# Second layer of a two-layer trunk: output projection by token halves, first products of the MLP and the input projection after it, operands ahead, stores on other queues

## The chip, the cores and the metric

The kernel runs on one core of a Trainium2 chip. The metric is the device time of one execution, in microseconds, as the median of three runs. The core has five engines that run their own instruction streams: TensorE (PE), VectorE (DVE), ScalarE (ACT), GpSimd (POOL) and SyncE (SP), which issues DMAs; ACT and POOL can issue DMAs too. They meet through semaphores, and each runs its instructions in the order of its stream.

## The reference

One sequence of 1024 tokens, model width 1024, float32. Layer 0 has attention, layer 1 a recurrent and convolution mixer; both end in an output projection. What matters here is the tail of each layer:

```
h = h + y @ w_out[i]                                   # output projection
hn = rms_norm(h, norm_mlp[i])
h = h + square(relu(hn @ w_mlp_in[i])) @ w_mlp_out[i]  # hidden width 4096
hn = rms_norm(h, norm_ple[i])
h = h + (p[i] @ w_ple_proj[i]) * sigmoid(hn @ w_ple_gate[i])   # p: 1024 x 256
...
return rms_norm(h, norm_final)
```

## The kernel before

Activations are held transposed: features on 128 partitions (8 blocks, `h[0]` to `h[7]`), 1024 tokens along the free axis, which splits into a left half (`lt`, tokens 0 to 511) and a right half (`rt`). `P` is 128, `H` 512, `T` 1024, `KB` 8.

Every float32 product is made of three matmuls of reduced operands (`mm3`, lines L95 to L97): an operand is split into a high part `xh` by ACT (`hi`, L76) and a low part `xl` by DVE (`lo`, L79 or L89 for weights, L155 with a gain), and PE adds high x high, high x low and low x high in one bank of its accumulator memory. Each matmul is 128 x 128 weights against 512 columns. Weights (`wr`, `raw`) come in blocks of 512 KB through two buffers, and their split parts (`wh`, `wl`) go through three.

The stages of layer 1, in order: the recurrent mixer; the output projection (`out_proj`, which calls `blocks`): 8 tiles of output features, two halves each; the norm (`rstd_full`) and `up_operands`; `mlp_up`; `mlp_down`; `ple_last`. Both parts of the MLP use seven products in place of eight (the Winograd form of Strassen's scheme, P1 to P7): `mlp_up` works on pairs of hidden tiles (16 pairs, index `mp`), and X1 to X7, sums and differences of quarters of the normed h, are its operands, `x10h` being the high part of block 0 of X1. A pair takes 84 matmuls, 12 for each product. Of its weights the sums `s12` and `s34` are split into `sh` and `sl`, and the last quarter into `ah`, `al`. A pair's results `z1` and `z2` (after relu and square) and the differences `tt` are stored to memory (`oa`, `ob`, `ot`), and `mlp_down` loads them again (`zr`), splits them into `zh` and `zl`, and runs each product over 8 steps `g` of 24 matmuls. When two products are complete, `h` gets their sums; a complete `h[m]` is stored (`hm`) and split for the last stage (`post`: `xh`, `xl`, `sq`, `acc`).

PE's order is the order in which the program issues matmuls. The other engines' instructions are ordered by a scheduler with priorities, and SP holds all loads and stores of these stages in one queue. In layer 0, attention's matmuls are mixed with filler by a planner (`at_run`, `fill`): the projections of the next heads, and at the end the one of layer 1's p with `w_ple_proj` (`("pp", 1, 0, 8, 7)`, 16 groups of 6 matmuls, whose operands are `ph`, its results `ppo`). They are stored in `pp` and read in `ple_last`.

Of the kernel before, what the change touches and what calls it, by code (L numbers as in the profile page):

```python
# [8 lines left out]
F32 = mybir.dt.float32  # L9
# [56 lines left out]
class Trunk:  # L66
# [95 lines left out]
    def run(self):  # L162
        tc, nc, A = self.tc, self.nc, self.A
        pool = tc.tile_pool
        with pool(name="w", bufs=1, side=LEFT) as self.wp, \
# [11 lines left out]
            for l in range(2):  # L177
                if l == 0:
                    self.attention(xp)
                with pool(name=f"md{l}", bufs=6, space=PSUM, reuse_waits="tile") as self.mx, ExitStack() as rs:  # L180
# [13 lines left out]
                    else:  # L194
                        hp = hs.enter_context(pool(name=f"h{l}", bufs=1, side=RIGHT, reuse_waits="tile"))
                        sp = self.ss.enter_context(pool(name=f"st{l}", bufs=1, side=RIGHT, reuse_waits="tile"))
                        h, xs, st = self.out_proj(l, xp, hp, None, sp)
                        nxt.close()
                        with pool(name=f"xo{l}", bufs=1, side=LEFT, reuse_waits="tile") as xo:
                            X = self.up_operands(l, h, st, sp, xo)  # L200
                            self.ss.close()
                            hs.close()
                            with pool(name=f"up{l}", bufs=1, side=RIGHT, reuse_waits="tile") as up:
                                self.mlp_up(l, X, up)
# [109 lines left out]
    def out_proj(self, l, xp, hp, xq, sp):  # L314
# [14 lines left out]
        def out(m, n, ps):  # L329
# [5 lines left out]
            if n:  # L335
                if xq is None:
                    nc.sync.dma_start(self.h1_d[m], h[m])
                else:
                    xs.append(self.xsplit(h[m], self.gain(3 * l + 1, m), xq))
                self.stat_block(st, h[m])  # L340
# [69 lines left out]
    def up_operands(self, l, h, st, sp, xo):  # L410

        nc = self.nc
        v = nc.vector
        lt, rt = slice(0, H), slice(H, T)
        if l:
            self.log_exp()
        r = self.rstd_full(st, sp, sp)
        X = {}

        def norm(k, s):  # L420
            v.scalar_tensor_tensor(h[k][:, s], h[k][:, s], self.gain(3 * l + 1, k), r[:, s], ALU.mult, ALU.mult)  # L421

        def put(p, k, full):
            X[p, k] = self.split(full, xo, (f"x{p}{k}h", f"x{p}{k}l"), 1)

        for k in range(4):
            norm(k, lt)
            put(1, k, h[k][:, lt])
        for k in range(4):
            norm(k + 4, lt)  # L430
            put(2, k, h[k + 4][:, lt])
        for k in range(4):
            a, b = h[k], h[k + 4]
            norm(k, rt)
            norm(k + 4, rt)
# [6 lines left out]
        for k in range(4):  # L442
# [3 lines left out]
            put(3, k, b[:, rt])  # L446
        for k in range(4):
            put(4, k, h[k + 4][:, lt])
        return X

    def mlp_up(self, l, X, up):

# [1510 lines left out]
```

## Time and profile before

| | us |
|---|---|
| median of 3 runs | 2649.96 (2648.81 to 2652.49) |
| the profiled execution | 2650.93, span 2649.2 |
| PE busy | 2525.4 (95%), 12296 matmuls |
| DVE busy | 1686.2 (64%) |
| ACT busy | 967.4 (37%) |
| POOL busy | 70.9 (3%) |

Busy is the time in which an engine executes; the rest it waits, for a semaphore or for nothing. The span is the profiled execution from its first to its last instruction. PE's time is far from even: the stages of layer 1 lie at about 1500 to 1742 us (recurrent mixer), 1742 to 1829 (output projection), 1885 to 2197 (`mlp_up`), 2204 to 2536 (`mlp_down`) and on to 2649 (`ple_last`).

### The profile page before, as it was taken

The page shows a single profiled execution, that of the slowest core. Times are in us where ns is not written, and L with a number is a line of the kernel's source. Part 1 is how long each engine was busy: PE and PEld are TensorE (multiplying, and loading weights), DVE is VectorE, ACT ScalarE, POOL GpSimd, SP SyncE. Part 2 cuts the span into 40 slices and gives each one's busy share as a digit, 9 for nine tenths or more (in the row PEclk, how much of TensorE's full clock was granted, in tenths as well). Part 3 has the DMA queues.
Part 4 walks back from the last instruction along what each step waited for, and adds up shares of the span by engine and source line. Part 5 has one row for each costly group of instructions (what it writes and reads, how often), then busy time and mean ns, then how long its engine had stood idle before and what let it go on. Part 6 is the DMA issues. An engine that isn't in the chain of part 4 may idle for free.

```text
span 2649.2 us, 32734 instructions
## 1 busy us (share of the span) xinstructions
PE 2525.4 (95%) x12296; PEld 2091.0 (79%) x12296; DVE 1686.2 (64%) x3214; ACT 967.4 (37%) x1508; POOL 70.9 (3%) x34
## 2 busy tenths in 40 slices
PE   8999999999999999999999999996599998999898
PEld 6788888888888888888888897885488887888677
DVE  6776756555856546645577678544766654667666
ACT  5554556553311211111134433322444444333445
POOL 1111110100000000000000000000000000000000
PEclk9999999999999999999999999998799999999899
DMA  5443433381122212212235655331144347678452
GB/s 172 114 120 108 136 85 91 106 280 68 37 72 84 76 56 76 84 60 72 84 106 200 193 180 176 134 146 47 65 146 170 132 156 296 242 246 284 137 177 94
DMA packets 158592, 351.77 MB, mean 133 GB/s; under 512 B 21600, under 2 KB 53600, under 8 KB 158432
## 3 DMA queue, kind: packets, MB, share of 16 engines
q1 hardware_dynamic: 158160, 349.40, 40.0%
q8 instruction: 97, 1.59, 0.2%
q14 instruction: 63, 0.52, 0.1%
q10 hardware_dynamic: 272, 0.26, 0.0%
HBM read 233.07 MB, written 90.18 MB: 122 GB/s over the span
## 4 chain that ended last, share of the span: by engine, by line
PE 87%; DVE 7%; ACT 2%; DMA 2%; issue 1%; SPq 1%; DVEq 0%; ACTq 0%
PE mm L95 26%; PE mm L96 26%; PE mm L97 26%; PE tp L1782 2%; PE S L1749 1%; PE S L1750 1%; PE o L1807 1%; PE o L1806 1%; DVE zl L79 1%; PE S L1874 1%; DMA x<-xT 0%; DVE p L1752 0%; DVE h L421 0%; DVE p L1771 0%; ACT p L1757 0%
## 5 line engine op out<-in xcount | busy, mean ns | idle before, releaser
L95 PE MATMUL mm<-xh,wh 128*128 128x512 f32 (+1 forms) x1504 | 587.1, 390 | 0.7 <-ACT xh L76 0.7
L96 PE MATMUL mm<-xl,wh 128*128 128x512 f32 (+1 forms) x1504 | 582.0, 387 | 2.6 <-DVE xl L155 2.6
L97 PE MATMUL mm<-xh,wl 128*128 128x512 f32 (+1 forms) x1504 | 583.9, 388 | 0.0
L76 ACT ACTIVATE wh<-wr 128x1024 fp32r<-128x1024 f32 (+1 forms) x159 | 167.4, 1053 | 558.8 <-PE mm L96 502.6
L96 PEld LDWEIGHTS mm<-xl,wh 128*128 128x128 f32 x1504 | 284.4, 189 | 63.4 <-DVE xl L155 3.4
L97 PEld LDWEIGHTS mm<-xh,wl 128*128 128x128 f32 x1504 | 284.2, 189 | 61.8
L95 PEld LDWEIGHTS mm<-xh,wh 128*128 128x128 f32 x1504 | 284.1, 189 | 59.7 <-ACT xh L76 1.1
L95 PE MATMUL mm<-hh,wh 128*128 128x512 f32 x512 | 203.8, 398 | 0.0
L97 PE MATMUL mm<-hh,wl 128*128 128x512 f32 x512 | 203.1, 397 | 0.0
L96 PE MATMUL mm<-hl,wh 128*128 128x512 f32 x512 | 203.1, 397 | 0.0
L95 PE MATMUL mm<-zh,wh 128*128 128x512 f32 x448 | 179.9, 402 | 17.7 <-ACT zh L76 17.7
L96 PE MATMUL mm<-zl,wh 128*128 128x512 f32 x448 | 179.7, 401 | 1.3 <-DVE zl L79 1.3
L97 PE MATMUL mm<-zh,wl 128*128 128x512 f32 x448 | 179.4, 400 | 0.0
L89 DVE TENSOR_TENSOR wl<-wr,wh 128x1024 fp32r<-128x1024 f32 x117 | 142.7, 1220 | 48.3 <-ACT wh L76 47.9
L381 DVE TENSOR_TENSOR h<-mm,h 128x512 f32<-128x512 f32 x128 | 88.3, 690 | 94.7 <-PE mm L97 93.3
L360 DVE TENSOR_TENSOR z<-mm,rstd 128x512 f32<-128x512 f32 x64 | 44.1, 691 | 149.9 <-PE mm L97 149.9
L1757 ACT ACTIVATE p<-p,m 128x128 f32<-128x128 f32 (+7 forms) x128 | 99.1, 775 | 100.5 <-DVE m L1752 99.6
L95 PEld LDWEIGHTS mm<-zh,wh 128*128 128x128 f32 x448 | 85.7, 191 | 39.3 <-ACT zh L76 18.5
L95 PEld LDWEIGHTS mm<-hh,wh 128*128 128x128 f32 x512 | 96.6, 189 | 24.6 <-issue 1.3
L97 PEld LDWEIGHTS mm<-hh,wl 128*128 128x128 f32 x512 | 96.5, 189 | 23.4
L96 PEld LDWEIGHTS mm<-hl,wh 128*128 128x128 f32 x512 | 96.6, 189 | 23.1
L95 PE MATMUL mm<-wh,xh 128*128 128x256 f32 x384 | 112.8, 294 | 2.1 <-DVE v L1505 1.4
(654 smaller groups left out, 4846.4 us busy)
## 6 DMA issues: line engine op xcount, KB each, us to landing
wr<-w_m SPq DMA_DIRECT2D x96, 512.0 KB, 3.3
raw<-w_m SPq DMA_DIRECT2D x80, 512.0 KB, 5.6
s<-s SPq DMA_DIRECT2D x64, 256.0 KB, 4.4
ot<-tt SPq DMA_DIRECT2D x32, 512.0 KB, 4.5
zr<-ot SPq DMA_DIRECT2D x32, 512.0 KB, 4.6
q<-zh SPq DMA_DIRECT2D x64, 128.0 KB, 2.3
ql<-zl SPq DMA_DIRECT2D x64, 128.0 KB, 2.3
pp<-ppo SPq DMA_DIRECT2D x32, 256.0 KB, 2.6
```

The source lines that it names most:

```text
L76: self.nc.scalar.activation(out, in_, AF.Copy, scale=scale)
L79: self.nc.vector.tensor_tensor(out, full, hi.bitcast(F32), ALU.subtract)
L89: self.weng.tensor_tensor(l, raw, h.bitcast(F32), ALU.subtract)
L95: mm(ps, L[0], R[0], start=first, stop=False)
L96: mm(ps, L[0], R[1], start=False, stop=False)
L97: mm(ps, L[1], R[0], start=False, stop=last)
L360: nc.vector.tensor_tensor(z, ps, r[0][:, s], ALU.mult)
L381: nc.vector.tensor_tensor(h[m][:, s], ps, h[m][:, s], ALU.add)
L1749: nc.tensor.matmul(S, qh, qk["k"][c][:, k], start=True, stop=False)
L1750: nc.tensor.matmul(S, ql, qk["k"][c][:, k], start=False, stop=True)
L1757: nc.scalar.activation(pt[:, :w], pt[:, :w], AF.Exp, bias=m, scale=-1.0, accum_out=den)
L1782: nc.tensor.transpose(tps[:, off + n * P : off + n * P + P], maps[j][:, kb * P : kb * P + P], self.ident)
```

## The change

It touches layer 1 and the end of attention in layer 0.

1. The last filler of attention is taken out. Its 96 matmuls are issued in the new `up_lead`, with all their copies and stores on ACT.
2. `out_proj_halves` computes all left halves and then all right halves of the output projection, loading the weights twice. During the right half the left half is normed (`rstd_half`, `norm_half`) and split into X1 and X2.
3. `up_lead` issues P1 and P2 of pairs 0 to 2 into banks of their own, then the projection of p. `up_operands` makes X3, X5 and X6, `up_first` issues P5 and P6 of pair 0 block by block, `up_rest` makes X4 and X7, and `mlp_up` goes on pair by pair.
4. The stores `oa` and `ob` are issued by ACT, the stores of h and `tt` by POOL; they were all issued by SP.
5. In `mlp_down` a generator makes the operands of each step up to two steps ahead (`more`), P3 comes before P7 in a step, the sums and posts of `h[0]` to `h[3]` are spread over the first steps of P4, and its last two steps run bank by bank.

The number of matmuls is the same, 12144 in the program.

```diff
+                        with pool(name=f"xa{l}", bufs=1, side=RIGHT, reuse_waits="tile") as xa:
+                            sp = self.ss.enter_context(pool(name=f"st{l}", bufs=1, side=RIGHT, reuse_waits="tile"))
+                            hp = hs.enter_context(pool(name=f"h{l}", bufs=1, side=RIGHT, reuse_waits="tile"))
+                            X = {}
+                            h, st = self.out_proj_halves(l, xp, hp, sp, xa, X)
+                            nxt.close()
+                            with pool(name=f"pp{l}", bufs=1, side=LEFT, reuse_waits="tile") as pl:
+                                lead = self.up_lead(l, X, st, sp, pl)
+                            with pool(name=f"xo{l}", bufs=1, side=LEFT, reuse_waits="tile") as xo:
+                                self.up_operands(l, h, st, xo, X)
+                                with pool(name=f"s0{l}", bufs=1, side=LEFT, reuse_waits="tile") as s0:
+                                    first = self.up_first(l, s0, lead, X)
+                                    self.up_rest(h, xo, X)
+                                    hs.close()
+                                    self.ss.close()
+                                    with pool(name=f"up{l}", bufs=1, side=RIGHT, reuse_waits="tile") as up:
+                                        self.mlp_up(l, X, up, s0, lead, first)
...
+    def out_proj_halves(self, l, xp, hp, sp, xa, X):
+        nc, A = self.nc, self.A
+        src = A["w_out"][l * KB : (l + 1) * KB]
+        ws = [self.wtile(src[j]) for j in range(3)]
+        ys, h, st = self.ys, {}, {"acc": None}
+        for k in (4, 5, 6, 7):
+            if k not in ys:
+                self.y_load(xp, k)
+        def mm(b, w, k, s):
+            self.mm3(b, self.cols(w)(k), (ys[k][0][:, s], ys[k][1][:, s]), k == 0, k == KB - 1)
+        def out(m, s, b):
+            if m not in h:
+                h[m] = hp.tile([P, T], F32, tag="h", bufs=KB, name="h")
+                nc.sync.dma_start(h[m], self.h_d[m])
+            nc.vector.tensor_tensor(h[m][:, s], b, h[m][:, s], ALU.add)
+            if st["acc"] is None:
+                st["acc"] = sp.tile([P, T], F32, tag="acc", bufs=1, name="acc")
+            if m == 0:
+                nc.scalar.activation(st["acc"][:, s], h[m][:, s], AF.Square)
+            else:
+                sq = sp.tile([P, H], F32, tag="z", bufs=4, name="sq")
+                nc.scalar.activation(sq, h[m][:, s], AF.Square)
+                nc.vector.tensor_tensor(st["acc"][:, s], st["acc"][:, s], sq, ALU.add)
+            nc.gpsimd.dma_start(self.h1_d[m][:, s], h[m][:, s])
         lt, rt = slice(0, H), slice(H, T)
+        bs = [self.bank() for _ in ws]
+        for part in (range(4), range(4, KB)):
+            for w, b in zip(ws, bs):
+                for k in part:
+                    mm(b, w, k, lt)
+        for m in range(3):
+            out(m, lt, bs[m])
+        for s in (lt, rt):
+            for m in range(3 if s is lt else 0, KB):
+                w, b = self.wtile(src[m]), self.bank()
+                for k in range(KB):
+                    mm(b, w, k, s)
+                out(m, s, b)
+                if s is rt and m == 0:
+                    self.log_exp()
+                    st["r"] = sp.tile([P, T], F32, tag="rstd", bufs=1, name="rstd")
+                    self.rstd_half(st, sp, lt)
+                if s is rt and m in (1, 2):
+                    for k in range(m * 4 - 4, m * 4):
+                        self.norm_half(l, h, st, k, lt)
+                        X[m, k % 4] = self.split(h[k][:, lt], xa, (f"x{k}h", f"x{k}l"), 1)
+        return h, st
+    def rstd_half(self, st, sp, s):
+        self.rstd_split(st["acc"][:, s], sp, H, ("z", "z", 4), ("z", "z", 4))(st["r"][:, s], D, EPS)
...
+    def up_lead(self, l, X, st, sp, pl):
+        nc, A = self.nc, self.A
+        lead = {}
+        ws = [self.wtile(A["w_m1"][l * FB + 2 * mp]) for mp in range(3)]
+        for mp in range(3):
+            for p in (1, 2):
+                lead[mp, p] = self.mx.tile([P, 512], F32, tag="mm", name="mm")
+                for k in range(4):
+                    c = slice(p * H - H + k * P, p * H - H + k * P + P)
+                    self.mm3(lead[mp, p], [o[:, c] for o in ws[mp]], X[p, k], k == 0, k == 3)
+            if mp == 0:
+                self.rstd_half(st, sp, slice(H, T))
+                xs = []
+                for k in range(2):
+                    raw = self.wp.tile([P, T], F32, tag="wr", bufs=2, name="praw")
+                    nc.sync.dma_start(raw, A["pT"][l, k])
+                    xs.append(self.split(raw, pl, (f"p{k}h", f"p{k}l"), 1))
+                w = [self.wtile(A["w_pp"][2 * l + j]) for j in range(2)]
+        for m in range(KB):
+            for n in range(2):
+                s = slice(n * H, n * H + H)
+                b = self.mp.tile([P, 512], F32, tag="mm", name="mm")
+                for k in range(2):
+                    c = slice(k * 512 + (m % 4) * P, k * 512 + (m % 4) * P + P)
+                    self.mm3(b, [o[:, c] for o in w[m // 4]], [o[:, s] for o in xs[k]], k == 0, k == 1)
+                t = pl.tile([P, H], F32, name="ppo", tag="ppo", bufs=4)
+                nc.scalar.copy(t, b)
+                nc.scalar.dma_start(self.pp_d[l][m][:, s], t)
+        return lead
...
+            self.norm_half(l, h, st, k, rt)
+            self.norm_half(l, h, st, k + 4, rt)
+            self.put(X, 3, k, b[:, rt], xo)
+            v.tensor_tensor(a[:, rt], a[:, rt], a[:, lt], ALU.subtract)
+            self.put(X, 5, k, a[:, rt], xo)
+            v.tensor_tensor(b[:, rt], b[:, rt], a[:, rt], ALU.subtract)
+            self.put(X, 6, k, b[:, rt], xo)
...
+            for p, s, x, y in ((4, lt, b[:, lt], b[:, rt]), (7, rt, b[:, rt], a[:, lt])):
+                v.tensor_tensor(b[:, s], x, y, ALU.subtract)
+                self.hi(X[p, k][0], b[:, s])
+                self.lo(X[p, k][1], b[:, s], X[p, k][0])
...
+        raw, a = self.up_raw(l, 0)
+        s12, ops = self.up_s12(a, s0)
+        for p in (6, 5):
+            lead[0, p] = self.mp.tile([P, 512], F32, tag="mm", name="mm")
+            for j, p in enumerate((5, 6)):
+                c = slice(j * H + k * P, j * H + k * P + P)
+                self.mm3(lead[0, p], [o[:, c] for o in ops], X[p, k], k == 0, k == 3)
+        return raw, a, s12
...
-                    nc.sync.dma_start(self.o1_d[g][:, e * H : e * H + H], z1[:, lt])
+                    nc.scalar.dma_start(self.o1_d[g][:, e * H : e * H + H], z1[:, lt])
...
-                    nc.sync.dma_start(two(self.o2_d[g]), both(z2))
+                    nc.scalar.dma_start(two(self.o2_d[g])[:, :, e, :], both(z2))
...
-                        nc.sync.dma_start(two(self.o4_d[g])[:, 2 * j : 2 * j + 2], both(t))
+                        nc.gpsimd.dma_start(two(self.o4_d[g])[:, 2 * j : 2 * j + 2, e, :], both(t))
...
+        def operands():
+            for p in (1, 2):
+                for g in range(8):
+                    yield wop(a(1, p, g)), zop(p, g)
...
+        def more(n):
+            while len(ahead) < n:
+                o = next(gen, None)
+                if o is None:
+                    return
+                ahead.append(o)
+
+        def step(banks, *flags):
+            more(2)
+            prod(banks, *ahead.pop(0), *flags)
+            more(2)
...
-            nc.sync.dma_start(self.h2_d[m], h[m])
+            nc.gpsimd.dma_start(self.h2_d[m], h[m])
...
+            step(b5, False, g == 7, True)
+            if g == 7:
+                for j in range(4):
+                    tt(h[j][:, rt], b5[j], h[j][:, rt], ALU.add)
+            step(b7, g == 0, g == 7)
         for j in range(4):
             tt(h[j][:, rt], u[j], h[j][:, rt], ALU.add)
             tt(u[j], b7[j], u[j], ALU.add)
-            for s in (lt, rt):
-                tt(h[4 + j][:, s], u[j], h[4 + j][:, s], ALU.add)
+        b4 = four()
+        for g in range(6):
+            step(b4, g == 0, False)
+            if g < 4:
+                post(g)
+                for s in (lt, rt):
+                    tt(h[4 + g][:, s], u[g], h[4 + g][:, s], ALU.add)
+
+        more(2)
         for j in range(4):
-            tt(h[j][:, rt], b5[j], h[j][:, rt], ALU.add)
-            post(j)
-        b4 = four()
-        for g in range(8):
-            prod(b4, wop(a(2, 2, g)), zop(4, g), g == 0, g == 7)
-        for j in range(4):
+            for i in range(2):
+                prod(b4, *ahead[i], False, i == 1, js=(j,))
             tt(h[4 + j][:, lt], b4[j], h[4 + j][:, lt], ALU.add)
             post(4 + j)
...
-        fill.append(("pp", 1, 0, 8, 7))
```

How instructions stand on three engines, before and after. First ACT, in layer 1 after the output projection. Before, the splits of the MLP operands follow the last of the norm's activations:

```order
L139 ACTIVATE rstd_16456<-rs_t_16480 128x512
L76 ACTIVATE x10h_16488<-h_16108 128x512
L76 ACTIVATE x11h_16493<-h_16115 128x512
...
L76 ACTIVATE x20h_16508<-h_16226 128x512
...
L76 ACTIVATE x30h_16592<-h_16226 128x512
L76 ACTIVATE x50h_16537<-t0_16529 128x512
L76 ACTIVATE x60h_16533<-t1_16530 128x512
L76 ACTIVATE x40h_16623<-h_16226 128x512
```

In the changed kernel the operands X3 and X5 to X7 follow the last copies and stores of the projection (`x_16704` is the high part of block 0 of X7):

```order
L499 COPY ppo_16677<-mm_16670 128x512
L500 DMA pp16_101<-ppo_16677 128x512
L499 COPY ppo_16687<-mm_16680 128x512
L500 DMA pp17_102<-ppo_16687 128x512
L499 COPY ppo_16697<-mm_16690 128x512
L500 DMA pp17_102<-ppo_16697 128x512
L76 ACTIVATE x30h_16722<-h_15937 128x512
L76 ACTIVATE x50h_16727<-h_15848 128x512
...
L76 ACTIVATE x63h_16780<-h_16051 128x512
...
L76 ACTIVATE x_16704<-h_15937 128x512
...
L76 ACTIVATE sh_16856<-s34_16853 128x1024
```

The copies `ppo` were in attention's stretch of ACT's stream and now stand ahead of `x30h`.

Next SP, where `mlp_up` ends and `mlp_down` begins. Before, the stores of the last pair stand between the first loads of `mlp_down`:

```order
L514 DMA oa7_190<-z1_18812 128x512
L559 DMA raw_18900<-w_m2 128x1024
L565 DMA zr_18906<-oa0_183 128x1024
L522 DMA ob7_198<-z2_18842 256x1x512
L529 DMA ot7_206<-tt0_18876 128x2x512
L529 DMA ot7_206<-tt1_18877 128x2x512
L559 DMA raw_18936<-w_m2 128x1024
L565 DMA zr_18942<-oa1_184 128x1024
```

In the changed kernel only loads stand there, behind the last weights of `mlp_up` and two of the last stage (`w_pg`):

```order
L537 DMA wr_18833<-w_m1 128x1024
L83 DMA wr_21258<-w_pg 128x1024
L83 DMA wr_21289<-w_pg 128x1024
L655 DMA raw_18990<-w_m2 128x1024
L661 DMA zr_18996<-oa0_183 128x1024
L655 DMA raw_19002<-w_m2 128x1024
L661 DMA zr_19008<-oa1_184 128x1024
L655 DMA raw_19038<-w_m2 128x1024
```

The four stores have gone to the streams of ACT and POOL; the order of the loads is unchanged.

Last DVE, in `mlp_down` from the sums of P3 and P7 on. Before (`zl_20840` belongs to P4's first step, `xl` and `acc` to the posts of `h[1]` to `h[3]`):

```order
L629 TENSOR_TENSOR h_19050<-mm_19507,h_19050 128x512
L79 TENSOR_TENSOR wl_20870<-raw_20867,wh_20869 128x1024
L155 SCALAR_TENSOR_TENSOR xl_20803<-h_19046,gains_69,xh_20802 128x1024
L297 TENSOR_TENSOR acc_20798<-acc_20798,sq_20806 128x1024
L155 SCALAR_TENSOR_TENSOR xl_20812<-h_19048,gains_69,xh_20811 128x1024
L297 TENSOR_TENSOR acc_20798<-acc_20798,sq_20815 128x1024
L155 SCALAR_TENSOR_TENSOR xl_20821<-h_19050,gains_69,xh_20820 128x1024
L297 TENSOR_TENSOR acc_20798<-acc_20798,sq_20824 128x1024
L79 TENSOR_TENSOR wl_20906<-raw_20903,wh_20905 128x1024
L79 TENSOR_TENSOR zl_20840<-zr_20837,zh_20839 128x1024
```

In the changed kernel:

```order
L79 TENSOR_TENSOR wl_20845<-raw_20842,wh_20844 128x1024
L79 TENSOR_TENSOR zl_20851<-zr_20848,zh_20850 128x1024
L748 TENSOR_TENSOR h_19158<-mm_19623,h_19158 128x512
L748 TENSOR_TENSOR h_19160<-mm_19624,h_19160 128x512
L748 TENSOR_TENSOR h_19162<-mm_19625,h_19162 128x512
L751 TENSOR_TENSOR h_19158<-u_18982,h_19158 128x512
L748 TENSOR_TENSOR h_19164<-mm_19626,h_19164 128x512
L79 TENSOR_TENSOR wl_20885<-raw_20882,wh_20884 128x1024
L79 TENSOR_TENSOR zl_20891<-zr_20888,zh_20890 128x1024
L752 TENSOR_TENSOR u_18982<-mm_20254,u_18982 128x512
L751 TENSOR_TENSOR h_19160<-u_18983,h_19160 128x512
L751 TENSOR_TENSOR h_19162<-u_18984,h_19162 128x512
```

The operands of the first two steps of P4 (`zl_20851`, `wl_20885`, `zl_20891`) now stand before or among the sums, and no post stands ahead of them.

## Rows read from the trace of the kernel before

**Rows 1.** The page: the chain that ended last, by engine.

```profile
PE 87%; DVE 7%; ACT 2%; DMA 2%; issue 1%; SPq 1%; DVEq 0%; ACTq 0%
```

**Rows 2.** Windows: us, busy PE, PEld, DVE, ACT, POOL, clock, DMA share, GB/s.

```profile
1850.00:1900.00 50.00, 15.08 (x54) 11.37 (x55) 38.53 (x60) 20.27 (x31) 0.00 (x0) 0.61 0.12 42
2600.00:2650.00 50.00, 38.72 (x319) 37.82 (x317) 35.86 (x83) 24.63 (x48) 3.81 (x3) 0.94 0.35 114
```

**Rows 3.** PE waits, 1700 to 2200 us, one of them: total us, times, longest.

```profile
PE mm L95 <- ACT x10h L76: 5.8, 1, 5.8
```

**Rows 4.** PE timeline, output projection to mlp_down: start, duration, instruction, idle before.

```profile
1827.82 0.40 PE L97 MATMUL mm<-xh,wl 128*128 128x512 f32 x1
...
1829.22 0.39 PE L97 MATMUL mm<-xh,wl 128*128 128x512 f32 x1
...
1884.87 0.79 PE L95 MATMUL mm<-x10h,wh 128*128 128x512 f32 x1 [41.04 <-ACT wh L76]
...
1892.25 0.50 PE L95 MATMUL mm<-x20h,wh 128*128 128x512 f32 x1
...
2196.43 0.39 PE L97 MATMUL mm<-x43h,al 128*128 128x512 f32 x1
2203.71 0.79 PE L95 MATMUL mm<-zh,wh 128*128 128x512 f32 x1 [6.89 <-ACT zh L76]
...
2209.82 0.53 PE L95 MATMUL mm<-zh,wh 128*128 128x512 f32 x1
```

**Rows 5.** Window of 10 us in the wait after the output projection.

```profile
1860.00:1870.00 10.00, 0.00 (x0) 0.00 (x0) 10.00 (x18) 5.69 (x10) 0.00 (x0) 0.50 0.00 0
```

**Rows 6.** DVE's groups between 1830 and 1886 us: form, count, busy us, mean ns.

```profile
L421 DVE SCALAR_TENSOR_TENSOR h<-h,gains,rstd 128x512 f32<-128x512 f32 x16 | 11.9, 745 | 0.0
L441 DVE TENSOR_TENSOR h<-h,t 128x512 f32<-128x512 f32 x4 | 2.7, 684 | 0.0
...
L79 DVE TENSOR_TENSOR sl<-sf,sh 128x1024 fp32r<-128x1024 f32 x2 | 2.4, 1224 | 0.0
```

**Rows 7.** Six windows of 10 us over attention's end: their sum.

```profile
sum 60.00, PE 55.57 PEld 48.01 DVE 40.55 ACT 37.99 POOL 0.00; mean PE 9.26 PEld 8.00 DVE 6.76 ACT 6.33 POOL 0.00
```

**Rows 8.** Timeline of PE over attention's end.

```profile
520.62 0.39 PE L95 MATMUL mm<-ph,wh 128*128 128x512 f32 x1
...
525.19 0.44 PE L1750 MATMUL S<-k,ql 128*128 128x128 f32 x1 [1.79 <-DMA ql<-zl]
...
577.81 0.39 PE L97 MATMUL mm<-ph,wl 128*128 128x512 f32 x1
```

**Rows 9.** Waits of DVE between 526 and 580 us.

```profile
DVE tl L79 <- ACT th L76: 7.0, 8, 1.8
DVE y L1855 <- ACT of L1854: 4.1, 5, 1.6
DVE p L1752 <- PE S L1750: 2.8, 4, 1.5
DVE den L1860 <- ACT p L1757: 2.4, 2, 1.3
```

**Rows 10.** DVE's copies of the input projection between 520 and 580 us.

```profile
L1403 DVE COPY ppo<-mm 128x512 f32<-128x512 f32 x8 | 5.4, 681 | 0.0
```

**Rows 11.** Timeline of PE from product P3 to the last stage.

```profile
2476.80 0.40 PE L97 MATMUL mm<-zh,wl 128*128 128x512 f32 x1
2487.99 0.79 PE L95 MATMUL mm<-zh,wh 128*128 128x512 f32 x1 [10.79 <-ACT zh L76]
...
2535.95 0.40 PE L97 MATMUL mm<-zh,wl 128*128 128x512 f32 x1
...
2551.46 0.40 PE L95 MATMUL mm<-xh,wh 128*128 128x512 f32 x1
```

**Rows 12.** Waits of SP's queue between 2150 and 2260 us.

```profile
SPq L514 <- ACT z L513: 37.4, 3, 13.5
```

**Rows 13.** The page: DMA issues, KB each, median us to landing.

```profile
ot<-tt SPq DMA_DIRECT2D x32, 512.0 KB, 4.5
```

More of the change, by code (lines that the diff above doesn't have):

```diff
@@ L432, in up_operands, with put @@
+    def put(self, X, p, k, full, xo):
+        X[p, k] = self.split(full, xo, (f"x{p}{k}h", f"x{p}{k}l"), 1)
+    def up_operands(self, l, h, st, xo, X):
+        v = self.nc.vector
+        lt, rt = slice(0, H), slice(H, T)
+        for p in (7, 4):
+            for k in range(4):
+                X[p, k] = [xo.tile([P, H], F32R, tag=f"x{p}{k}{x}", bufs=1, name="x") for x in "hl"]
         for k in range(4):
             a, b = h[k], h[k + 4]
-            norm(k, rt)
-            norm(k + 4, rt)
@@ L453, in mlp_up @@
+    def mlp_up(self, l, X, up, s0, lead, first):
         nc, A = self.nc, self.A
@@ L485, in zt @@
                 return z[j]
-            g, e = mp // 2, mp % 2
-            def mm(p, k):
-                b = {1: 1, 2: 1, 6: 6, 5: 5, 3: 5, 7: 7, 4: 7}[p]
-                if b not in bank:
-                    bank[b] = self.bank()
-                ks = slice(k * P, k * P + P)
-                self.mm3(bank[b], [o[:, ks] for o in w[p]], X[p, k], k == 0 and p == b, k == 3, p != b)
+            if mp > 2:
+                put((1, 2), self.split(raw[0], self.wp, ("wh", "wl"), 3))
+            if s12 is None:
+                s12, ops = self.up_s12(a, s0)
+                put((5, 6), ops)
+            s34 = up.tile([P, 1024], F32, tag="sf", bufs=1, name="s34")
+            tt(s34[:, lt], a[0], a[2], ALU.subtract)
+            tt(s34[:, rt], a[1], s12[:, rt], ALU.subtract)
+            put((7, 3), self.split(s34, up, ("sh", "sl"), 1))
+            put((4,), self.split(a[3], up, ("ah", "al"), 2))
             def out(p):
@@ L569, in wop, with prod @@
             return self.split(full, self.wp, ("wh", "wl"), 3)
-        def prod(banks, w, z, first, last, more=False):
-            for j in range(4):
+        def prod(banks, w, z, first, last, more=False, js=range(4)):
+            for j in js:
                 for e in range(2):
@@ L590, in mlp_down @@
             for g in range(8):
-                w = wop(a(1, p, g))
-                prod(b1, w, zop(p, g), p == 1 and g == 0, g == 7, p == 2)
+                step(b1, p == 1 and g == 0, g == 7, p == 2)
                 if p == 1 and g in (3, 4):
```

151 lines of the change are left out of this document (58 added, 93 removed).

## The prediction

> **What bounds the kernel now.** I read the chain first: 87% of the path that ended last is PE [rows 1]. So only what makes PE start a matmul later counts, and a faster store or another engine's work matters where PE waits for it. The windows say where that is: between 1850 and 1900 us PE is busy for 15.08 of 50 us and the granted clock is 0.61, near the lower of its two levels (1.2 of 2.4 GHz) [rows 2]. PE waits 41.04 us there for ACT wh before the matmul at 1884.87 [rows 4], and 5.8 us for ACT x10h a little earlier [rows 3]. This is the norm and the making of the MLP operands after the output projection, with DVE as the engine behind it: 18 of its instructions fill 10.00 of 10 us while PE has none [rows 5].
>
> How much a place loses I take from PE's timeline: matmuls counted in program order, times their pitch, against the time that passed.
> - Pitch: six steps from 1827.82 to 1829.22 us are 0.233 us each in the output projection; the 1,319 steps from 1892.25 (the 25th matmul of mlp_up) to 2196.43 (its last, the 1,344th) are 0.2306 us each [rows 4]. In mlp_down I use 0.234.
> - Output projection to the end of mlp_up: 2196.43 - 1829.22 = 367.2 us for 1,344 x 0.2306 = 309.9 us of matmuls: 57.3 us lost [rows 4]. The first 24 of mlp_up ran from 1884.87 to 1892.25, 7.4 us for 5.5: 1.9 us of that is the lower clock after the wait.
> - mlp_up to mlp_down: 2209.82 is the 13th matmul after 2196.43; 13 x 0.234 = 3.0 of 13.4 us: 10.4 lost, 6.89 of it in the wait for zh; the twelve from 2203.71 on took 6.1 us for 2.8 [rows 4].
> - P3/P7 to the end of P4 in mlp_down: 2535.95 - 2476.80 = 59.2 us for 192 x 0.234 = 44.9: 14.2 lost, 10.79 of it one wait for ACT zh [rows 11].
> - mlp_down to the last stage: 2551.46 is the 37th matmul after 2535.95; 8.7 of 15.5 us: 6.9 lost [rows 11].
>
> **The change part by part.**
>
> Attention. 96 matmuls (32 triples) leave the stretch from 520.62 to 577.81 us [rows 8]: 96 x 0.233 = 22.4 us of PE work. Attention's own chain (S, p on DVE and ACT, transposition, th, tl, o) stays, so not all of it comes back. At the low end only DVE's eight copies vanish, 5.4 us [rows 10], and every wait of DVE between 526 and 580 us (7.0 + 4.1 + 2.8 + 2.4 = 16.3 us) stays [rows 9]. At the high end DVE never waits: 40.55 us of its work in the 60 us [rows 7] less 5.4 are 35.1, and the 4.6 us at the start (520.62 to 525.19), where PE waits for ql to come back from memory [rows 8], remain: 39.7 of 57.4 us, 17.7 back. I take the middle, **12 us**, since about half of the waits are for th and S, which PE would deliver sooner. The end 0 stays in the range for the clock (a rival).
>
> Output projection. Same matmuls in another order; eight more loads and splits of weights run beside them. Right half: after m = 1 DVE has 20 instructions 512 wide (norms, lows and sums of X1 and X2) ahead of the lower part of the weights of m = 4. At 0.62 us each, between the 0.556 of 18 in 10 us [rows 5] and the 0.68 and 0.745 of single rows [rows 6], plus 0.7 and 1.22 for h and the split [rows 6] that is 14.3 us, where PE has two tiles of 5.6 and a first pair of matmuls, 0.5. **Loses 2.8 us** (0 to 6).
>
> Lead and up_first. PE gets the P1 and P2 of three pairs (72 x 0.2306 = 16.6 us), which hide the norm of the right half, then the 96 of the projection (22.4 us). But on ACT all sixteen copies of that projection stand ahead of x30h (the ACT rows in the part on the change), so X3, X5 and X6 start only after its last matmul: 1.9 us (the last copy and two highs at 0.62 each) and then 18 DVE instructions of 0.62: x63l is ready 13.1 us after that matmul and up_first done at 13.6, with 24 x 0.2306 = 5.5 us of work: 8.1 us lost. Behind it on DVE stand 14 instructions of X4 and X7, four for the next weights and u2, and the lower split sl of 1.22 [rows 6], which pair 0's P7 needs: 14 x 0.62 + 4 x 0.66 + 1.22 = 12.5, so ready at 25.6; PE has two matmuls to do from 13.6 on, 0.5 us: 11.5 us lost. The clock then costs 1.9 us as it does now. Sum 21.5. So this stretch takes 309.9 + 22.4 + 21.5 = 353.8 instead of 367.2 us: **13.4 us gained** (8 to 21; at 0.556 an instruction the walk is 3 us shorter, at 0.70 it is 4 longer).
>
> Stores on other queues. SP's three waits for z before the store oa are the longest of its queue, 13.5 us, with loads behind them [rows 12]. In the change the loads stand in front, yet the first raw still waits for its buffer until P7 of the last pair, the first zr for the last up matmul, and wh and zh stand on ACT behind the last z2. Walking load, zh and its matmul I get 5.6 us after the last up matmul, against 6.89: **1 us gained** (0 to 10, if the walk is wrong). By the Trainium skill, "DMA: Bandwidth & Descriptors", section "Issuing engines are not separate DMA queues", queues of several engines end on the same 16 engines and only issue time is saved; the sum by that rule would have 0 here instead of 1. No run yet shows which holds.
>
> mlp_down. The operands of P4 now stand before the sums of h, so the 10.79 us wait for zh should go, with the slow restart. The posts (xl, acc and two sums) move into its first four steps: DVE has four wide instructions of 1.22 [rows 6] and two of 0.62, 6.1 us, in a step of 24 x 0.234 = 5.6, but by the order of its rows it is some 5 us ahead when P4's third step comes. Of 14.2 us I count **12 gained** (5 to 14). At the end the last two g run bank by bank, so three of the four h are summed before the last matmul. From the third bank's end, 2.8 us before it, DVE has two sums of h at 0.68 and seven wide instructions (three xl, two sums of squares, two gate splits) at 1.22, 9.9 us: the last xl is ready 7.1 us after the last matmul, where 22 matmuls take 5.1. With that 2 us and some clock lost of 6.9, **4 gained** (0 to 6.9).
>
> Sum: 12 - 2.8 + 13.4 + 1 + 12 + 4 = 39.6 us. The profiled execution took 2650.93 us (its span 2649.2), 1.0 above the median of the runs: 2650.9 - 39.6 = 2611.3, **2611 us**.
>
> **The rivals.**
> - The waits hide better than I walk them: attention returns 17.7 and the 10.4 us at mlp_down's start go as well. 2611 - 6 - 9 = 2596. For it: the loads no longer queue behind stores. Against: zr needs the last hidden block, whoever issues it.
> - Attention returns nothing: without its filler its latency stays as it is, and PE's clock drops. 2611 + 12 = 2623; if 33 us of PE work ran at the lower clock for a third of the time, 2630. For it: PE already waits for ql at 525 us [rows 8], with filler ahead of it. Against: from 2600 to 2650 us PE is busy 38.72 of 50 us, in pieces, and the clock stays at 0.94 [rows 2]; attention's end would have 55.57 - 22.4 = 33.2 us [rows 7] in some 45.
> - The wait in mlp_down only moves: splits and posts on ACT and DVE collide in P4's first steps and nothing of the 12 comes back: 2623.
> - Slower: GpSimd's stores. Each pair writes two tt tiles (512 KB each) and DVE may write the next pair's only when they have landed, 84 x 0.2306 = 19.4 us later. Issued by SP they land in 4.5 us [rows 13]; GpSimd issues none now, so nothing here shows its time. From a landing of 19.4 us on, each us costs up to 14 us over 14 pairs; past 22.7 us, five times the row, it eats the 40 us and 5 more: then 2656 or above. The Trainium skill, "SBUF — State Buffer", section "Who interferes with whom", has this mechanism: descriptors of GpSimd's DMAs are starved by DVE in its two-port modes. The instructions in question are nearly all tensor_tensor, which by that section does not take what they need.
>
> **How the numbers follow.** My forecast holds 0.49, the better-hidden case 0.18, attention giving nothing 0.16, the wait that moves 0.10, slower stores 0.07. The likeliest gives 2611. Its own bounds, taken as independent (6, 7, 7, 3, 3 us), reach about 12 us to each side; the cases at 2596 and 2623 to 2630 belong in the range: 2594 to 2632, with under 2 in 10 outside. A measurement of this kernel tells some 0.2% (5.3 us) from no change. Every case but the last is faster by more; I leave something for several bounds falling together: faster 0.90, same 0.04, slower 0.06.
>
> **What would show it.** Right: PE waits after the output projection fall from some 51 us to under 25, and those left are for ACT x50h/x6.h and for sh or sl of pair 0, at half the granted clock; a wait of 2 to 3 us for wl in the right half; no wait over 3 us before P4; attention ends 8 to 16 us earlier; the wait at mlp_down's start is still over 4 us. Wrong: waits of DVE for GpSimd's stores in every pair, attention's end with the clock near 0.5, or operands of P4 late again.

## The result and the profile after

The changed kernel takes **2615.31 us** (median of 4 runs, 2612.82 to 2619.48) against 2650.26 for the kernel before on the same chip: ratio 0.9869, 95% interval 0.9852 to 0.9886. The forecast was 2611, its range 2594 to 2632. The profiled execution took 2615.06 us with a span of 2613.2, 36.0 less than before; PE is busy for 97% of it instead of 95%, and most of the chain is still PE's (compare [rows 1]):

```profile
PE 88%; DVE 6%; ACT 2%; issue 1%; DMA 0%; SPq 0%; DVEq 0%; ACTq 0%
```

The long wait after the output projection [rows 4] is gone. The windows of the kernel after (us, then busy PE, PEld, DVE, ACT, POOL, clock, DMA share, GB/s) answer to [rows 2] and [rows 5]; the last stage now lies 32 to 37 us earlier, so its window is taken 40 us earlier:

```profile
1850.00:1900.00 50.00, 36.09 (x127) 26.62 (x126) 31.15 (x49) 26.43 (x43) 0.00 (x0) 0.83 0.28 100
2560.00:2610.00 50.00, 40.84 (x330) 39.37 (x329) 38.06 (x87) 27.23 (x52) 3.81 (x3) 0.95 0.34 111
1870.00:1880.00 10.00, 8.54 (x22) 5.73 (x21) 10.00 (x18) 5.16 (x9) 0.00 (x0) 0.66 0.00 0
1880.00:1890.00 10.00, 0.12 (x1) 0.12 (x1) 9.91 (x18) 6.00 (x10) 0.00 (x0) 0.72 0.05 10
```

DVE still fills 20 us between 1870 and 1890, and PE is without work for 11.3 us of these, where it was for 41 in one piece. PE's timeline of the kernel after (start, duration, instruction, idle time before and what ended it) has the same places as [rows 4, 8, 11]:

```profile
523.09 0.45 PE L1879 MATMUL S<-k,ql 128*128 128x128 f32 x1 [1.80 <-DMA ql<-zl]
...
540.11 0.55 PE L1935 MATMUL o<-th,v 128*128 128x256 f32 x1 [3.63 <-DVE y L1984]
...
570.90 0.47 PE L95 MATMUL mm<-xh,wh 128*128 128x512 f32 x1
...
1802.92 0.79 PE L97 MATMUL mm<-xh,wl 128*128 128x512 f32 x1 [2.74 <-DVE wl L89]
...
1826.10 0.39 PE L97 MATMUL mm<-xh,wl 128*128 128x512 f32 x1
...
1865.85 0.40 PE L97 MATMUL mm<-p1h,wl 128*128 128x512 f32 x1
1868.47 0.50 PE L95 MATMUL mm<-x50h,sh 128*128 128x512 f32 x1 [2.23 <-ACT x50h L76]
...
1889.88 0.80 PE L95 MATMUL mm<-x,sh 128*128 128x512 f32 x1 [10.23 <-ACT sh L76]
...
1891.14 0.80 PE L97 MATMUL mm<-x,sl 128*128 128x512 f32 x1
...
2180.19 0.39 PE L97 MATMUL mm<-x,al 128*128 128x512 f32 x1
2186.47 0.80 PE L95 MATMUL mm<-zh,wh 128*128 128x512 f32 x1 [5.90 <-ACT zh L76]
...
2192.28 0.39 PE L95 MATMUL mm<-zh,wh 128*128 128x512 f32 x1
...
2504.12 0.40 PE L97 MATMUL mm<-zh,wl 128*128 128x512 f32 x1
2511.21 0.50 PE L96 MATMUL mm<-xl,wh 128*128 128x512 f32 x1 [1.56 <-DVE xl L155]
...
2514.58 0.39 PE L95 MATMUL mm<-xh,wh 128*128 128x512 f32 x1
```

From these rows the gain is cut at matmuls that both kernels have: the first S that waits for ql, the first matmul of layer 0's output projection, the last of the recurrent mixer (1739.27 before, 1731.41 after) and of layer 1's output projection, the last of `mlp_up`, the 13th of `mlp_down` and its last, the 37th of the last stage.

| stretch | before, us | after, us | gain | forecast |
|---|---|---|---|---|
| attention's end, from ql on | 53.5 | 47.8 | 5.7 | 12 |
| output projection | 89.95 | 94.7 | -4.7 | -2.8 |
| from there to the last of `mlp_up` | 367.2 | 354.1 | 13.1 | 13.4 |
| on to the 13th of `mlp_down` | 13.4 | 12.1 | 1.3 | 1 |
| on to its last (P4) | 326.1 | 311.8 | 14.3 | 12 |
| on to the 37th of the last stage | 15.5 | 10.5 | 5.05 | 4 |

These are 34.7 of 36.0 us. Of the rest 2.1 lie ahead of ql, where the code differs by the filler's operands and its first three matmuls (0.7 us), and -0.9 behind the last row. What lies ahead of ql differs by more between executions of one order (last section), so the 2.1 can't be put down to the change.

### The profile page after: what moved, and what is told of

Read it like the earlier page. It is cut to its first block, busy times and chain, and to the rows that moved or that the text cites. A ratio compares the mean times of both kernels' runs of the same rounds, so it can differ in the third digit from the quotient of the medians.

```text
span 2613.2 us, 32842 instructions
## 1 busy us (share of the span) xinstructions
PE 2527.2 (97%) x12296; PEld 2090.7 (80%) x12296; DVE 1693.9 (65%) x3225; ACT 978.9 (37%) x1531; POOL 102.6 (4%) x88
## 4 chain that ended last, share of the span: by engine, by line
PE 88%; DVE 6%; ACT 2%; issue 1%; DMA 0%; SPq 0%; DVEq 0%; ACTq 0%
PE mm L95 27%; PE mm L97 27%; PE mm L96 27%; PE tp L1911 2%; PE S L1878 1%; PE S L1879 1%; PE o L1936 1%; PE o L1935 1%; DVE zl L79 1%; PE S L2003 1%; DVE p L1881 1%; DVE p L1900 0%; DVE tl L79 0%; DMA ql<-zl 0%; PE mm L1115 0%
## 5 line engine op out<-in xcount | busy, mean ns | idle before, releaser
L76 ACT ACTIVATE wh<-wr 128x1024 fp32r<-128x1024 f32 (+1 forms) x167 | 175.8, 1054 | 557.0 <-PE mm L96 480.8
L89 DVE TENSOR_TENSOR wl<-wr,wh 128x1024 fp32r<-128x1024 f32 x130 | 158.6, 1221 | 52.2 <-ACT wh L76 51.4
L97 PE MATMUL mm<-wh,xl 128*128 128x256 f32 x384 | 109.7, 286 | 0.0
```

The lines of the kernel that those rows point to most:

```text
L76: self.nc.scalar.activation(out, in_, AF.Copy, scale=scale)
L89: self.weng.tensor_tensor(l, raw, h.bitcast(F32), ALU.subtract)
L97: mm(ps, L[1], R[0], start=False, stop=last)
```

## The experiments

All ran beside the kernel before, whose medians were 2648.7 to 2650.3 us. In the ratios 0.0015, or 4 us, is about the half width of an interval; a difference between two of these kernels is so clear of the scatter from some 6 us on (an estimate: 4 us times the root of 2), and smaller ones rest on the traces.

**The projection of p back in attention.** The filler returns and leaves `up_lead`; all else stays.

```diff
-                w = [self.wtile(A["w_pp"][2 * l + j]) for j in range(2)]
-        for m in range(KB):
-            for n in range(2):
...
-                nc.scalar.copy(t, b)
-                nc.scalar.dma_start(self.pp_d[l][m][:, s], t)
+        fill.append(("pp", 1, 0, 8, 7))
```

> The changed kernel with the projection of p back in attention as filler; all else stays. Mine: the move was a net loss. In the lead its 96 matmuls take 22.4 us and its copies on ACT hold x30h back, and attention gave only 7.8 us for them. Without them the first x30l is ready about 20 us after the output projection instead of 42, so from there to the end of mlp_up 334 us instead of 354, attention ends 7.8 us later: 2603 us. Rival: the projection fills time in which PE would wait anyway; then this stretch keeps its 354 us less at most a few, and the kernel is 7.8 us slower: 2623 us.

Measured: **2598.56 us**, ratio 0.9808 (0.9794 to 0.9823), so this part of the change costs 16.7 us. PE's timeline of this run:

```profile
520.98 0.45 PE L1864 MATMUL S<-k,ql 128*128 128x128 f32 x1 [1.95 <-DMA ql<-zl]
...
574.87 0.48 PE L95 MATMUL mm<-xh,wh 128*128 128x512 f32 x1
...
1830.11 0.40 PE L97 MATMUL mm<-xh,wl 128*128 128x512 f32 x1
...
1847.60 0.39 PE L95 MATMUL mm<-x50h,sh 128*128 128x512 f32 x1
...
1872.02 0.79 PE L95 MATMUL mm<-x,sh 128*128 128x512 f32 x1 [9.74 <-ACT sh L76]
...
2161.35 0.39 PE L97 MATMUL mm<-x,al 128*128 128x512 f32 x1
```

Attention's end takes 53.9 us, 6.1 more than in the kernel after. From the output projection to the last of `mlp_up` it is 331.2 instead of 354.1 us: 22.9 less, and the 96 matmuls are 22.4 us of work. Behind the lead (P1 and P2 of pairs 0 to 2) they covered nothing. The 72 matmuls of the lead alone last until x50h is there: `up_first` starts at 1847.60 with no wait. DVE then makes four of the eight blocks of the norm during `up_first`, which loses 8.7 us to its pace and the clock; with the projection ahead the norm is done before, but x50h is late, and 7.9 us are lost. The wait for sh is there with and without them.

**The projection ahead of P1 and P2.** The same groups, their operands and weights stand first in `up_lead`, so that ACT's copies are done before x30h is due; the sums of `rstd_half` are issued at m = 2.

```diff
+        w = [self.wtile(A["w_pp"][2 * l + j]) for j in range(2)]
+        for m in range(KB):
+            if m == 2:
+                self.rstd_half(st, sp, slice(H, T))
...
         ws = [self.wtile(A["w_m1"][l * FB + 2 * mp]) for mp in range(3)]
         for mp in range(3):
...
-            if mp == 0:
-                self.rstd_half(st, sp, slice(H, T))
```

> The changed kernel with the projection of p ahead of P1 and P2 of the three pairs instead of behind them. Mine: the copies on ACT are done 23 us after the output projection, X3, X5 and X6 are ready at 35, up_first (from 39 on) waits for nothing and only P7 of pair 0 waits, about 3 us: the stretch takes 336 us instead of 354, 2597 us. Rival: not ACT's copies but DVE's own chain of norms and splits is what up_first and P7 wait for; then the waits of 2.2, 10.2 us and the lower clock stay and the time is 2613 to 2617 us.

Measured: 2609.77 us, ratio 0.9851 (0.9837 to 0.9866). My size was wrong, the named waits were right: none of `up_first` is left and sh's is shorter, but a new one stands at the front, where the split of w_pp is late. PE's timeline of this run:

```profile
1830.67 0.79 PE L95 MATMUL mm<-p0h,wh 128*128 128x512 f32 x1 [6.72 <-ACT wh L76]
...
1882.68 0.79 PE L95 MATMUL mm<-x,sh 128*128 128x512 f32 x1 [4.40 <-ACT sh L76]
```

The stretch to the last of `mlp_up` takes 349.6 us, 4.5 less than after. By the medians alone, 5.5 us apart, this would not be clear.

**Half of the projection in attention.** m = 0 to 3 as filler, m = 4 to 7 behind the lead.

```diff
+        fill.append(("pp", 1, 0, 4, 7))
-        for m in range(KB):
+        for m in range(4, KB):
```

> Half of the input projection (m = 0 to 3, 48 matmuls, 11.2 us) goes back into attention's end, the other half stays behind the lead. Theory: attention's end is a chain of latencies of about 48 us (47.8 without filler, measured from the matmul that waits for ql) with some 14 us of holes, so half of the filler costs it nothing: 47.8 to 49 us there, and the lead's stretch loses 11.2 us against the kernel after. 2615.3 - 11.2 = 2604 us. Rival: filler delays the chain in proportion, 6.1 us for the whole and 3 for the half: an end of 50.9 us and 2607 us.

Measured: 2607.76 us, ratio 0.9839 (0.9823 to 0.9856). Behind the lead, half costs 12.0 us (343.25 against 331.2). Attention's end takes 49.9 us, between the two theories: the first half costs 2.1 us there, the second 4.0. With the scatter of this end between executions (last section) that doesn't tell the two apart; it does show that most of such filler is free in attention, and behind the lead none: the whole costs 6.1 of its 22.4 us there, or 9.4 against the shortest end without filler (44.5 us), so 58 to 73% of it is free.

**All stores on SP again.** `oa`, `ob`, `ot` and those of h issued by SP, in the order of the changed kernel's program.

```diff
-                    nc.scalar.dma_start(self.o1_d[g][:, e * H : e * H + H], z1[:, lt])
+                    nc.sync.dma_start(self.o1_d[g][:, e * H : e * H + H], z1[:, lt])
...
-                        nc.gpsimd.dma_start(two(self.o4_d[g])[:, 2 * j : 2 * j + 2, e, :], both(t))
+                        nc.sync.dma_start(two(self.o4_d[g])[:, 2 * j : 2 * j + 2, e, :], both(t))
```

> The changed kernel with all stores of layer 1's MLP back in SP's queue. Mine: the queue of a store costs little, since what mlp_down's first step waits for is the last hidden block: the wait at its start goes from 5.9 to 7 us, a few more loads come late, 2615 to 2620 us. Rival: other queues are what keeps the loads in time all through mlp_up; then waits for weights appear in many pairs and the time is over 2625 us.

Measured: 2621.44 us (2613.9 to 2622.64), ratio 0.989 (0.9874 to 0.9906). The intervals of this kernel and of the change overlap; the trace shows the place. It is of the fastest of the four executions (2613.9 us). My time was near, my wait was not: 13.90 us where I had 7. The rival's waits for weights aren't there: PE has none in `mlp_up` from pair 1 on. PE's timeline of this run, `mlp_up` to `mlp_down`:

```profile
2172.57 0.39 PE L97 MATMUL mm<-x,al 128*128 128x512 f32 x1
2186.86 0.80 PE L95 MATMUL mm<-zh,wh 128*128 128x512 f32 x1 [13.90 <-ACT zh L76]
```

SP's queue in this run, then in the kernel after (`raw` and `zr` hold what the first step of `mlp_down` splits):

```profile
2176.22 0.52 SPq L625 DMA_DIRECT2D ob<-z  x1
2176.95 1.56 SPq L632 DMA_DIRECT2D ot<-tt  x2
2178.61 1.07 SPq L655 DMA_DIRECT2D raw<-w_m  x1
2179.77 1.15 SPq L661 DMA_DIRECT2D zr<-oa  x1
```

```profile
2174.43 0.33 SPq L655 DMA_DIRECT2D raw<-w_m  x1
2180.61 0.33 SPq L661 DMA_DIRECT2D zr<-oa  x1
```

zr is issued 7.2 us after the last matmul of `mlp_up` with the stores on SP and 0.4 us after it without. 3.65 us pass until `ob` has the last z2, with the loads behind it; `ob` and `ot` take 2.1 us to issue, and then comes the first `raw`, which the kernel after issues 5.8 us ahead of its last matmul of `mlp_up`. The wait for zh grows by 8.0 us. The rule of the Trainium skill that I cited ("DMA: Bandwidth & Descriptors", "Issuing engines are not separate DMA queues": only issue time is saved) doesn't count what a store that waits holds up in its queue. The trace doesn't agree with it here: 2.1 us of issue were saved, and 8.0 us of wait.

**Only the new `mlp_down`,** put into the kernel before.

> The kernel before with the new mlp_down alone (operands ahead, P3 before P7, posts spread, last steps by bank, its stores on GpSimd). Mine: the 14.3 and 5.0 us that the profile after shows in mlp_down and at the last stage come from this part by itself: 2631 us. Rival: they need the stores on other queues in mlp_up, whose tail runs into mlp_down; then less than half comes, over 2640 us.

Measured: 2631.12 us, ratio 0.993 (0.9914 to 0.9947). From the 13th matmul to the end of P4 it takes 313.5 us instead of 326.1, and the last stage takes the 10.5 us of the change. This part stands alone.

**X7 ahead of X4.** On the kernel with the projection in attention, pair 0's s34 is split in `up_first`, into free buffers of the weights, and X7 is made before X4.

```diff
-            for p, s, x, y in ((4, lt, b[:, lt], b[:, rt]), (7, rt, b[:, rt], a[:, lt])):
+        for p, f in ((7, lambda a, b: (a[:, rt], b[:, rt], a[:, lt])), (4, lambda a, b: (b[:, lt], b[:, lt], b[:, rt]))):
+            for k in range(4):
```

> The projection stands in attention as in the run with it put back (2598.6 us), and the operands of pair 0's P7 come first: its weights' sums s34 are split ahead of the last operands, and the four blocks of X7 are made ahead of those of X4. Theory: the 9.74 us wait for sh is DVE's walk over 14 instructions of X4 and X7 and the split of s34; by the new order P7 can run behind X7 at DVE's pace and end about 6 us after the last x63l instead of 15, less 1.3 us by which the split delays x63l: 7 us less, 2591.5 us, and no wait for sh over 2 us. Rival: DVE's total is what PE waits for and the 7 us come back as waits for X4 before P4: 2597 to 2599 us.

Measured: 2601.95 us, ratio 0.9819 (0.9805 to 0.9834): no gain, as the rival had it (the time is 3 us above its range), though not for its reason (below).

**The norms of X1 and X2 spread** over m = 1 to 4 of the right half, on the kernel with the projection in attention.

```diff
-                if s is rt and m in (1, 2):
-                    for k in range(m * 4 - 4, m * 4):
+                if s is rt and 1 <= m <= 4:
+                    for k in range(m * 2 - 2, m * 2):
```

> The projection stands in attention as in the run with it put back (2598.6 us), and the norms and splits of X1 and X2 are issued two blocks at each of m = 1 to 4 instead of four at m = 1 and 2. Theory: the wait for wl in the right half (2.74 us, with about 2 us of half clock behind it) is the burst of 20 instructions of DVE; halved it fits beside PE's tiles, and the output projection takes 90 us again instead of 94.7: 2594.5 us. Rival: the wait is for the transfer or the copy that makes wh, and it stays: 2598.6 us.

Measured: **2593.25 us** (2591.64 to 2595.57), ratio 0.9791 (0.9775 to 0.9808). The wait for wl is gone and the output projection takes 90.4 us where it took 94.9 with the projection of p put back, so the burst on DVE was its cause. These 4.5 us are the gain that the trace shows; the medians are 5.3 apart.

**Both edits.**

> Both edits of the two runs before together, on the kernel with the projection in attention. If the two waits are independent the gains add: 2598.6 - 7 - 4 = 2587.5 us. Rival: DVE's work before P7 is one sum, and what the right half gains is lost behind the lead: 2591 us.

Measured: 2592.9 us, ratio 0.979 (0.9775 to 0.9804): what the spread gives alone. PE's longest wait between 1800 and 1900 us (total us, times, longest) and its place in the timeline, P7's first matmul, show why X7 gave nothing:

```profile
PE mm L95 <- ACT u L588: 8.9, 1, 8.9
1867.06 0.79 PE L95 MATMUL mm<-x,wh 128*128 128x512 f32 x1 [8.86 <-ACT u L588]
```

P7 no longer waits for sh (the run with X7 alone has the same wait of 8.86 us). It waits for a bank, of which there are eight: the P1 and P2 of three pairs and P5 and P6 hold them all, and the first is freed by ACT's copy u1 (L588), whose tile lies in h's memory, in use until X4 is made.

**u1, u2 and u5 of pair 0 ahead of X4,** in buffers of the weights, on the kernel with both edits.

```diff
+        u = [self.wp.tile([P, 1024], F32, tag=x, bufs=3, name="u") for x in ("wh", "wl")]
+        self.nc.scalar.copy(u1, lead[0, 1])
...
+            if p == 7:
+                v.tensor_tensor(us[1], lead[0, 6], us[0], ALU.add)
+                v.tensor_tensor(us[2], lead[0, 5], us[1], ALU.add)
```

> The kernel of the run with both edits (2592.9 us), and in it pair 0's u1, u2 and u5 get buffers of the weights, so that u1 is copied out of its bank and u2 and u5 are made before X4, instead of behind it when h's memory is free. Theory: in that run P7 had its operands and waited 8.86 us for a bank that u1's copy empties; now P7 runs behind X7, P3 behind u5 and P4 behind X4, and the three end about 8 us earlier, of which 4 are lost again before pair 1's P6, whose sums s12 stand behind all of it on DVE: 2589 us, and no wait over 2 us before P7. Rival: DVE's total work until pair 1 is the bound, and the whole 8.86 us come back as waits for pair 1's sh or sl: 2592 to 2593 us.

Measured: 2600.37 us, ratio 0.9816 (0.98 to 0.9832). Worse by 7.5 us (by the ratios 6.9), which neither theory said. PE's timeline of this run:

```profile
1862.24 0.79 PE L95 MATMUL mm<-x,wh 128*128 128x512 f32 x1
...
1873.70 0.47 PE L95 MATMUL mm<-x,ah 128*128 128x512 f32 x1 [2.43 <-DVE z L612]
...
1881.79 0.63 PE L95 MATMUL mm<-x60h,sh 128*128 128x512 f32 x1 [3.91 <-ACT sh L76]
...
1884.61 0.80 PE L97 MATMUL mm<-x60h,sl 128*128 128x512 f32 x1 [1.76 <-DVE sl L79]
```

P7 starts at once, 1.3 us after x63l's matmul. Pair 1's first matmul comes 20.8 us after that of x63l; with both edits alone it came after 20.45 (1856.97 to 1877.42). The wait has moved to P4 and pair 1, and in pieces it costs more clock: of the 98 steps from x63l's matmul to the first of pair 2, 28 are between 0.38 and 0.70 us apart instead of 0.23, with both edits alone 10. These steps take 38.95 us instead of 34.13, and that is all by which the stretch to the last of `mlp_up` is longer (336.2 us, 331.4 before). Of what the two profiled executions differ by beyond it, 3.7 us lie ahead of ql, where no code differs.

**A second bank for o,** in the kernel after, once attention has no filler left.

```diff
+        if self.o3 is not None and w == 256:
+            self.on = (self.on + 1) % 4
+            return (self.o2, self.o3)[self.on % 2][:, self.on // 2 * 256 : self.on // 2 * 256 + 256]
```

> The kernel after, with a second bank for the attention products o once no filler is left: one of the two banks that the filler used. Theory: the missing half of what attention should have given back (6 of 12 us) is the single o bank, which y must empty first: PE waited 8.9 us for y in 5 places. With two banks these waits go, attention's end takes 42 to 44 us instead of 47.8, and the kernel 2610 us. Rival: th, tl and p, which ACT and DVE make in turn, set the pace, the waits move to tl and p, and the time stays at 2613 to 2616 us.

Measured: 2606.3 us (2603.7 to 2609.39), ratio 0.9844 (0.9829 to 0.9859). PE's timeline of this run:

```profile
522.51 0.30 PE L1885 MATMUL S<-k,ql 128*128 128x128 f32 x1 [1.64 <-DMA ql<-zl]
...
563.65 0.47 PE L95 MATMUL mm<-xh,wh 128*128 128x512 f32 x1
```

Attention's end takes 41.1 us, 12.4 less than before. PE's waits between 523 and 564 us:

```profile
PE S L2009 <- ACT rden L1997: 3.1, 3, 1.9
PE mm L1942 <- DVE tl L79: 1.3, 3, 0.6
PE tp L1917 <- ACT p L1892: 1.0, 1, 1.0
PE o L1942 <- DVE tl L79: 0.4, 2, 0.2
```

None is for y. Attention's end isn't the same in every execution: with the change's own order it took 47.8, 47.9 and, in the run with the stores on SP, 44.5 us. The waits for y are 7.9 us in all three, so it isn't they that differ; the clock does (last section). The bank is so worth 3.4 to 6.8 us of trace, and by the ratios, whose intervals overlap, 6.6 us. The planner knows of the bank and issues these matmuls in another order; the run doesn't part the two.

## Why the prediction was right, and where not

The forecast, its sign and most of its terms held. No rival came whole, but attention gave less than half of its term, and with a lower clock, as one of them had it. Point by point:

- **Attention: mis-sized, 5.7 us for 12.** I took the middle of the bounds 5.4 and 17.7 because "PE would deliver sooner" what DVE waits for. The result lies at the low bound, and the sign that attention would end 8 to 16 us earlier wasn't met (7.8, of which 2.1 lie ahead of ql). Waits between 524 and 572 us in the kernel after, to be read against [rows 9]:

```profile
DVE tl L79 <- ACT th L76: 9.0, 8, 2.9
PE o L1935 <- DVE y L1984: 7.9, 4, 3.6
...
DVE p L1881 <- PE S L1879: 3.1, 7, 1.1
```

  DVE's waits for th and S are not shorter (7.0 and 2.8 before). What I didn't walk is the bank of o: without filler PE comes to the next o before y has emptied it, and waits 7.9 us. The second bank took these waits away, and there DVE waits less for th as well:

```profile
DVE tl L79 <- ACT th L76: 3.4, 8, 0.8
```

  That the stretch came to my 12 with it is in part luck, since I hadn't the bank in the walk. The clock took a share too, which I had left to a rival. A window of the kernel before, with filler, then three of the kernel after:

```profile
540.00:550.00 10.00, 9.00 (x57) 7.71 (x56) 6.81 (x18) 6.30 (x14) 0.00 (x0) 1.00 0.89 291
530.00:540.00 10.00, 6.08 (x45) 5.34 (x43) 8.10 (x25) 7.24 (x17) 0.00 (x0) 0.97 0.53 213
540.00:550.00 10.00, 9.89 (x54) 9.56 (x55) 5.65 (x15) 4.53 (x9) 0.00 (x0) 0.69 0.77 288
550.00:560.00 10.00, 6.73 (x36) 5.64 (x36) 6.12 (x16) 5.52 (x13) 0.00 (x0) 0.83 0.53 184
```

  After a window with 6.08 busy us the granted clock falls to 0.69, a mean between its levels, and 54 matmuls fill 9.89 us; with filler 57 took 9.00 us at 1.00. How much of the missing 6.3 us is the bank and how much the clock isn't shown.

- **Output projection: -4.7 for -2.8.** The wait for wl of m = 4 is 2.74 us, as walked (the terms of the walk, 14.3 less 11.7, make 2.6). I left out the clock: the seven steps from 1802.92 to 1805.96 us take 3.04 us where 1.63 would do, 1.4 more. The spread norms removed both.

- **Lead and `up_first`: 13.1 for 13.4, and the steps as walked.** x30h stands behind the last copy on ACT, while DVE stands idle. ACT's and DVE's timelines of the kernel after:

```profile
1866.28 0.59 ACT L499 COPY ppo<-mm 128x512 f32<-128x512 f32 x1 [0.82 <-PE mm L97]
...
1867.27 0.63 ACT L76 ACTIVATE x30h<-h 128x512 fp32r<-128x512 f32 x1 [0.40 <-ACT ppo L499]
```

```profile
1867.93 0.69 DVE L79 TENSOR_TENSOR x30l<-h,x30h 128x512 fp32r<-128x512 f32 x1 [15.72 <-ACT x30h L76]
```

  From the projection's last matmul to P7's third, the first that needs sl, are 25.3 us (1865.85 to 1891.14), 25.6 in my walk. Of the rest of the loss, 1.0 us lies ahead of it, which I had at nothing, and 1.7 behind it, where I had 1.9 for the clock. But the sum hides what the move of the projection is worth: I priced its 22.4 us of work and 21.5 us of loss, and the loss is just as large without it (331.2 - 309.9 = 21.3). Its covering value there is nil. Had I priced the stretch without the move as well, my own terms (12 back in attention for 22.4 paid here) would have said that it loses 10. It lost 16.7.

- **Stores on other queues: 1.3 for 1, but for another reason than the number suggests.** The walk behind zr (5.90 us for 5.6) was right. Before, SP's order had the first zr ahead of `ob` and `ot`; in the new order of the program the same queue would have cost 8 us. The part is worth that within this change and little against the kernel before. GpSimd's stores, the slower rival, are no trouble (compare [rows 13]):

```profile
ot<-tt POOLq DMA_DIRECT2D x32, 512.0 KB, 5.2
```

  5.2 us from issue to landing, far from 19.4, and SP's took 4.5. By the Trainium skill, "SBUF — State Buffer", section "Who interferes with whom", DVE in its two-port modes locks GpSimd out of the ports that they share and so starves it of time to write a DMA's descriptors; tensor_tensor has no such mode and takes only the read side of the pair. The trace agrees: all of DVE's work between 1900 and 2180 us is tensor_tensor, and the stores landed in 5.2 us.

- **`mlp_down`: 14.3 for 12; last stage: 5.05 for 4.** The wait of 10.79 us [rows 11] is gone and none takes its place: all 14.2 us lost there came back. Of the last stage a wait of 1.56 us for xl is left, where I had 2.

Against the terms of the 39.6 us the stretches differ by -6.3, -1.9, -0.3, +0.3, +2.3 and +1.05; with 2.1 ahead of ql and -0.9 behind that gives the 36.0 us of the span. So near a total is in part luck: 8.5 us too little in three terms and 3.65 too much in three others offset each other.

## What to carry to other kernels

In these runs filler paid where the chain of other engines is longer than PE's work, and was paid in full where it isn't: price a moved piece at both ends, by what the stretch loses with and without it. Here it hid 58 to 73% of itself in attention and nothing behind a lead that already lasted until the first operand was there; the change without that move, with a burst on DVE spread over four tiles, takes 2593 us in place of 2615. Before operands are made earlier, ask what the matmuls would wait for next: a bank (X7 ahead of X4: 9.74 us for sh became 8.86 for a bank), then the next pair's operands. A store that waits for its data costs its queue more than its issue.

## What the runs showed of the hardware

- A single wait of 2.74 us was followed by 3 us of matmuls 0.43 us apart instead of 0.23 (from 1802.92 in the kernel after), and busy time doesn't show the clock: in the run with u1 ahead of X4 PE was busy for 9.32 of 10 us between 1860 and 1870 us, but at a granted clock of 0.58 and with 23 matmuls, where the window 1840 to 1850 us of the kernel after, at 1.00, has 45.
- Two executions with the same order in attention differ by up to 3.4 us in its end (44.5 and 47.9 us) and by more in what lies ahead of ql (518.8 to 523.1 us without filler, 520.6 to 525.8 with it). What goes with the shorter end is the granted clock: in the four windows of 10 us from the first S that waits for ql on, it was 0.69, 0.82, 0.84 and 0.83 where the end took 47.8 us, 0.68, 0.83, 0.83 and 0.83 for 47.9, and 0.83, 0.85, 0.98 and 1.00 for 44.5. The program of attention and the waits for y are the same in all three; why the clock differs isn't shown. Gains of a stretch are to be read between matmuls of that stretch, not from absolute times.
